# Two of the sixteen weight casts of a fused tanh-multiply matmul are given to VectorE alone

## The chip, the cores and the metric

The kernel runs on one core of a Trainium2 chip, in one launch. The metric is device time in microseconds (us), the median of several runs. Inputs and output lie in the chip's main memory (HBM) as float32.

The engines have these names in the profile: PE is TensorE (matmul), PEld its weight loads, ACT is ScalarE, DVE is VectorE, POOL is GpSimd, SP is SyncE, which here only issues DMAs.

## The reference

```python
def reference(x, w1, w2):          # x: 16 x 512 x 1024, w1 and w2: 1024 x 768
    y1 = np.matmul(x, w1)
    y2 = np.matmul(x, w2)
    return (np.tanh(y1) * y2).astype(np.float32)
```

Flattened, x has 8192 rows: 64 row tiles of 128. The contraction is 1024 = 8 slices of 128.

## The kernel before

**Tiling.** Each weight (`t` = 0 for w1, 1 for w2) is loaded in eight slices of 128 x 768 and cast from float32 to float16 into one tile `wh`. A slice's 768 columns are taken as F = 512 columns and G = 256. A matrix product accumulates eight slices in one of the eight PSUM banks (`bank0` to `bank7`).

**Stages.** The six row tiles 0 to 5 (`HEAD`) and the last (`TAIL`) are computed in the plain way (line 449 issues each matmul, lines 455 and 459 the tanh and the multiplication). The 57 tiles between are taken three at a time, in 19 rounds. Each round computes the three tiles by 15 half-depth products instead of 18, on sums of blocks of x (`A_SUMS`, VectorE, line 434) and on sums of blocks of the weights made once (`B_SUMS`, VectorE, line 424). The products are line 477, the copies and additions between them lines 483 and 492, tanh and multiplication lines 495 and 500. `C_OPS` and `PE_ORDER` fix the order of the products.

**Head.** x tiles 0 to 3 come as float32 and are transposed on PE (line 351). ScalarE moves them out of PSUM with a cast (line 342). PE then goes through the weight slices in the order of their arrival: for every slice `k` it issues F of tiles 0 to 3 (four matmuls of 512 columns) and G of tiles 0 to 3 (four of 256), first for w1 (pass 0), then for w2 (pass 1). Two tiles share a bank for G. So pass 0 holds six banks until ScalarE's tanhs `thF0` to `thF3`, `thG0` to `thG3` have read them, and pass 1 needs six banks itself. Tiles 4 and 5 come as float16 through a casting DMA of GpSimd's queue (line 384) and are transposed on PE (line 361); later tiles are transposed by a DMA (line 387).

**Weights.** The slices are called `a0` to `a7` (w1) and `b0` to `b7` (w2). `a0` to `a3` are loaded by ScalarE's queue, the rest by SyncE's, in order (line 338), through twelve buffers. The casts, `ca0` to `cb7`, are line 344 where VectorE makes them and line 342 where ScalarE does (the same helper `copy`).

**Sums of magnitudes.** ScalarE also sums the absolute values of each x tile (`D0` to `D63`) and of each cast slice (`awa0` to `awb7`), both at line 390. At the end they decide whether the float16 results may stand or a slower general path has to run. GpSimd reuses an x buffer only when its `D` is done.

**Who runs what, and when.** Nothing of the order is written by hand apart from the products of the rounds. A `Planner` holds every operation with the engines that may run it and a time for each, with its due time and its needs. It plays the whole program forward with those assumed times. Where an operation has two engines it is given to the one that can begin earlier, or that is taken first. PSUM banks are dealt in the same play to whatever asks next (`bank_free`). The instructions are then recorded in the order of the planned starts, engine by engine, and kept in that order (`pin`). A cast is entered as `{"dve": 0.5, "act": 0.74}`. Among operations of one engine that could start now or soon, the one with the earlier due time goes first. A cast's due time is `6 + 1.3 * k + 9.5 * t`, that of a tanh of pass 0 is 20, that of `aw` 80 or more.

In the order planned for the kernel before, VectorE has `ca0` to `ca4`, `cb4`, `cb5`, `cb6`, and ScalarE `ca5` to `ca7`, `cb0` to `cb3` and `cb7`.

Of the kernel before, what the change touches and what calls it, by code (L numbers as in the profile page):

```python
# [77 lines left out]
class Planner:  # L78
# [13 lines left out]
    def op(self, name, engines, due, needs, fn, *args, behind=(), issued=(), chains=(), xfer=0.0, latency=None, seeds=False):  # L92


        assert name not in self.ops, name
        self.ops[name] = dict(engines=engines, due=due, needs=[n for n in needs if n], behind=[n for n in behind if n], issued=[n for n in issued if n], fn=fn, args=args,
                              chains=chains, xfer=xfer, latency=latency, seeds=seeds)
        for c in chains:
            self.chains.setdefault(c, {"left": 0, "bank": None, "end": 0.0, "by": ""})["left"] += 1
# [134 lines left out]
def kernel(  # L234
# [29 lines left out]
    LOW, HIGH = 512.0, 1024.0  # L264
    XT_BUFS, S_BUFS, O_BUFS, C_BUFS, WF_BUFS = 4, 2, 3, 2, 12
    WARM = 21
    AFTER = (0, 0, 0)
    SOON = {"S": 3.0, "D": 3.0}
    GATE = 2
# [41 lines left out]
    op = plan.op  # L311
# [229 lines left out]
    for n, what in enumerate(loads):  # L541
# [5 lines left out]
        else:  # L547
            t = "ab".index(what[0])
# [1 line left out]
            op(f"L{what}", {"sp": 0.05}, 0.1 * n - 100, [], load_w, t, i, nc.scalar if what in early else nc.sync,  # L550
               issued=[before], behind=[f"c{slices[j][0]}{slices[j][2]}" if j >= 0 else ""], xfer=xfer)
    for a, t, k in slices:
        op(f"c{a}{k}", {"dve": 0.5, "act": 0.74}, 6 + 1.3 * k + 9.5 * t,
           [f"L{a}{k}"], cast_w, t, k)
        op(f"aw{a}{k}", {"act": 0.92}, 80 + 10 * (t * KO + k), [f"c{a}{k}"], abs_w, t, k)
    for mt in range(4):
# [155 lines left out]
    for mt in range(MT - TAIL - 3):  # L712
        op(f"st{mt}", {"sp": 0.05}, 52 + 4.33 * mt if mt >= HEAD else 250 + 5 * mt, outs[mt], store, mt,
           issued=[f"T{MT - 1}"] if mt < HEAD else [f"p{AFTER[(mt - HEAD) % 3]}.{(mt - HEAD) // 3 + 1}"], xfer=1.1)
    for mt in range(4, MT):
# [23 lines left out]
    pin(nc.vector.memset(ones, 2.0 ** -12))  # L739
    for n in range(WARM):  # L740
        pin(nc.tensor.matmul(banks[n % 8][:, n // 8 % 2 * 2 * P:][:, :2 * P], ones.bitcast(bf16)[:, :P], ones.bitcast(bf16), start=True, stop=True))
# [106 lines left out]
```

## Time and profile before

| | us |
|---|---|
| median of four runs | 300.5 (300.26 to 300.64) |
| the profiled execution, its own time | 300.65 |
| its span, from the first instruction to the last | 298.9 |
| PE busy | 292.1 |
| DVE busy | 240.3 |
| ACT busy | 219.8 |
| POOL busy | 32.9 |

The profile is of one execution. Its span lies inside its own time, so about 1.75 us of that time are outside what the rows show. A row of a timeline gives start, duration, engine, line, operation, written tile <- read tiles, shapes and the number of instructions merged into it. What stands in square brackets is the idle time of the engine before it and what ended that. PE's matmuls overlap: a row's duration is drawn longer than the time from one start to the next. A 512-column matmul is drawn with 0.38 us and starts 0.22 us after the one before it, a 256-column one with 0.27 and 0.11 us.

The granted clock of TensorE is 0.999 over the span. The twelve weight slices of SyncE's queue land, by the trace's stamps, at 13.13, 14.12, 15.12, 16.09 (`a4` to `a7`), 17.05, 18.04, 20.15, 21.13, 22.11, 23.11, 24.06 and 25.19 us (`b0` to `b7`).

### The profile page before, as it was taken

Reading aid. Unit: us, or ns where it says so; the run is one execution under the profiler, and the core shown is the slowest. Engines: PE = TensorE matmul, PEld = TensorE weight load, DVE = VectorE, ACT = ScalarE, POOL = GpSimd, SP = SyncE. Lnnn points to the kernel's source line nnn. Section 1 sums busy time; section 2 is a strip of 40 time slices with the busy share of each in tenths; the row PEclk is TensorE's granted clock in tenths of the full one; section 3 lists DMA queues with packets and bytes.
Section 4 is the critical chain, followed back from the end, with each engine's and each line's share of the span. In section 5 each row is a group of like instructions: output and inputs, shape, how many; then the busy total and the mean of one; then the engine's idle time right before and its main releaser. Section 6 shows DMA issues by size and latency. Waiting matters only on the chain.

```text
span 298.9 us, 4459 instructions
## 1 busy us (share of the span) xinstructions
PE 292.1 (98%) x1418; PEld 138.9 (46%) x1418; DVE 240.3 (80%) x497; ACT 219.8 (74%) x438; POOL 32.9 (11%) x67
## 2 busy tenths in 40 slices
PE   7999999999999999999999999999999999999994
PEld 5656544444444444444444444444444444444452
DVE  1208999988988887888978979797898988888854
ACT  3779989999786868767777767777766777773640
POOL 0021211211101101110110111011011101000000
PEclk9999999999999999999999999999999999999999
DMA  7999999999999999999999999999999999994053
GB/s 281 408 400 210 162 167 152 176 197 244 210 221 206 232 226 145 252 286 147 249 165 274 209 173 252 178 238 198 242 203 194 228 185 267 172 391 158 19 230 124
DMA packets 82585, 64.79 MB, mean 217 GB/s; under 512 B 63617, under 2 KB 64129, under 8 KB 82561
## 3 DMA queue, kind: packets, MB, share of 16 engines
q1 hardware_dynamic: 73344, 47.20, 63.7%
q0 software_dynamic: 8640, 15.73, 36.2%
q10 hardware_dynamic: 576, 1.57, 1.3%
q8 instruction: 11, 0.18, 0.3%
q14 instruction: 14, 0.11, 0.1%
HBM read 39.85 MB, written 25.17 MB: 218 GB/s over the span
## 4 chain that ended last, share of the span: by engine, by line
PE 91%; DMA 6%; ACT 0%; ACTq 0%; DVE 0%; SPq 0%; issue 0%
PE bank L477 82%; PE bank L449 8%; DMA w_f<-in_w_dram 6%; ACTq L338 0%; PE bank L361 0%; ACT wh L342 0%; ACT o L455 0%; DVE o L459 0%; SPq L338 0%; PE bank L515 0%
## 5 line engine op out<-in xcount | busy, mean ns | idle before, releaser
L477 PE MATMUL bank<-b,s 128*128 128x512 f16 x608 | 140.9, 379 | 0.0
L477 PEld LDWEIGHTS <-s 128*128 128x128 f16 x760 | 74.3, 98 | 89.6
L492 DVE TENSOR_TENSOR bank<-bank,s 128x512 f32<-128x512 f32 x95 | 66.0, 695 | 29.2 <-ACT s L483 22.2
L483 ACT ACTIVATE s<-bank 128x512 f32<-128x512 f32 x95 | 55.3, 597 | 42.2 <-PE bank L477 39.3
L390 ACT ACTIVATE junk<-xh 128x1024 f16<-128x1024 f16 x60 | 63.3, 1055 | 0.2
L500 DVE TENSOR_TENSOR o<-o,bank 128x256 f32<-128x256 f32 (+1 forms) x114 | 60.5, 546 | 2.3 <-ACT o L495 1.7
L477 PEld LDWEIGHTS <-xT 128*128 128x128 f16 x380 | 37.2, 98 | 44.7 <-issue 0.2
L477 PE MATMUL bank<-b,xT 128*128 128x512 f16 x228 | 55.4, 379 | 0.0
L384 POOL DMA_DIRECT2D xh<-in_x_dram x60 | 32.1, 535 | 197.9 <-ACT junk L390 149.8
L495 ACT ACTIVATE o<-bank 128x256 f32<-128x256 f32 x76 | 33.1, 437 | 10.1 <-DVE bank L492 6.5
L449 PE MATMUL bank<-wh,xT 128*128 128x512 f16 (+1 forms) x208 | 38.8, 338 | 1.0 <-ACT xT L342 0.7
L477 PE MATMUL bank<-wh,xT 128*128 128x512 f16 x152 | 39.0, 379 | 0.0
L477 PE MATMUL bank<-wh,s 128*128 128x512 f16 x152 | 39.0, 379 | 0.0
L434 DVE TENSOR_TENSOR s<-s,xT 128x512 f16<-128x512 f16 x76 | 31.6, 415 | 0.0
L449 PEld LDWEIGHTS <-xT 128*128 128x128 f16 x208 | 20.0, 98 | 17.9 <-ACT xT L342 1.4
L483 ACT ACTIVATE bank<-bank 128x512 f32<-128x512 f32 x38 | 20.4, 579 | 8.9 <-PE bank L477 7.2
L495 ACT ACTIVATE o<-s 128x512 f32<-128x512 f32 x38 | 23.9, 628 | 2.2 <-DVE s L492 2.0
L344 DVE CAST wh<-w_f 128x768 f16<-128x768 f32 x8 | 4.5, 564 | 18.6 <-DMA w_f<-in_w_dram 18.6
L434 DVE TENSOR_TENSOR s<-xT,xT 128x512 f16<-128x512 f16 x38 | 15.8, 416 | 0.0
L434 DVE TENSOR_TENSOR s<-xT,s 128x512 f16<-128x512 f16 x38 | 15.8, 416 | 0.0
L492 DVE TENSOR_TENSOR bank<-s,bank 128x512 f32<-128x512 f32 x19 | 13.1, 691 | 2.6 <-ACT o L495 2.5
L390 ACT ACTIVATE junk<-wh 128x768 f16<-128x768 f16 x16 | 13.6, 848 | 0.2
(39 smaller groups left out, 121.7 us busy)
## 6 DMA issues: line engine op xcount, KB each, us to landing
out_dram<-o SPq DMA_DIRECT2D x60, 384.0 KB, 4.6
xh<-in_x_dram POOLq DMA_DIRECT2D x60, 256.0 KB, 6.1
w_f<-in_w_dram SPq DMA_DIRECT2D x12, 384.0 KB, 8.1
x_f<-in_x_dram SPq DMA_DIRECT2D x4, 512.0 KB, 7.1
w_f<-in_w_dram ACTq DMA_DIRECT2D x4, 384.0 KB, 7.6
out_dram<-o SPq DMA_DIRECT2D x4, 256.0 KB, 2.5
xT<-xh SPq DMA_TRANSPOSE x58, 5.6
out_dram<-o SPq DMA_DIRECT2D x4, 128.0 KB, 2.1
```

The source lines that it names most:

```text
L344: pin(engine[e].tensor_copy(dst, src))
L384: pin(nc.gpsimd.dma_start(xhs[mt], xf[mt]))
L390: pin(nc.scalar.activation(junk[:, :src.shape[-1]], src, ACT.Abs, scale=scale, accum_out=sums[:, column:column + 1]))
L434: pin(engine[e].tensor_tensor(ss[i, v], x_operand(i, a), x_operand(i, b), OP[how]))
L449: pin(nc.tensor.matmul(b, xts[mt][:, k, :], rhs, start=first, stop=k == KO - 1, skip_group_check=True))
L477: pin(nc.tensor.matmul(place(i, dst), x_operand(i, a)[:, k, :], w_rhs(b, k), start=begins and k == 0, stop=k == KH - 1, skip_group_check=T ...
L483: pin(nc.scalar.activation(d, place(i, src), ACT.Copy, scale=float(sign)))
L492: pin(nc.vector.tensor_tensor(d, a, b, ALU.add if signs == (1, 1) else ALU.subtract))
L495: pin(nc.scalar.activation(out_tile(HEAD + 3 * i + r)[:, lo:lo + n], place(i, src)[:, :n], ACT.Tanh, scale=float(sign)))
L500: pin(nc.vector.tensor_tensor(o, o, place(i, src)[:, at:at + n], ALU.mult))
```

## The change

One constant is added, and the casts of w2's slices with k = 2 and 3 (`cb2` and `cb3`) are entered with VectorE as their only engine. In line 553 of the kernel before, `t` is 1 for w2.

```diff
@@ -264,6 +264,7 @@
     LOW, HIGH = 512.0, 1024.0
     XT_BUFS, S_BUFS, O_BUFS, C_BUFS, WF_BUFS = 4, 2, 3, 2, 12
     WARM = 21
+    ON_DVE = (2, 3)
     AFTER = (0, 0, 0)
@@ -550,7 +551,7 @@
     for a, t, k in slices:
-        op(f"c{a}{k}", {"dve": 0.5, "act": 0.74}, 6 + 1.3 * k + 9.5 * t,
+        op(f"c{a}{k}", {"dve": 0.5} if t and k in ON_DVE else {"dve": 0.5, "act": 0.74}, 6 + 1.3 * k + 9.5 * t,
            [f"L{a}{k}"], cast_w, t, k)
```

Since the planner plays the program anew, more than two casts move. The orders that it gives (`B` is a sum of weight blocks, `S` of x blocks, `mu` a multiplication of the head, `T4` and `T5` the copies of the transposed tiles 4 and 5 out of PSUM; `01F2` is row tile 0, w2, F, slice 2; line numbers behind line 266 are one higher than before):

```
ACT before: ca5 ca6 ca7 cb0 cb1 cb2 cb3 thF0..3 thG0..3 cb7 awa3 D4..D8 D0..D3 thF4 thM4 awa4 ...
ACT after:  ca5 ca6 ca7 cb0 cb1 awa3 thF0..3 thG0..3 cb6 cb7 awa4 D4..D8 D0..D3 thF4 thM4 awa5 ...
DVE before: ca0..ca4 cb4 cb5 cb6 B5 B6 B36 T4 B24 B37 muF0 muF1 T5 muF2 muF3 ...
DVE after:  ca0..ca4 cb2 cb3 cb4 cb5 B5 B6 B36 B24 T4 B37 B26 muF0 muF1 T5 muF2 muF3 ...
PE before:  01F0 11F0 01F1 11F1 01F2 21F0 11F2 21F1 31F0 21F2 01G0 31F1 11G0 21G0 01G1 31G0 ...
PE after:   01F0 11F0 21F0 31F0 01F1 01G0 11F1 11G0 21F1 21G0 31F1 31G0 01G1 11G1 21G1 31G1 01F2 ...
```

PE's order is the same in both from slice 3 of pass 1 on, to the end. SyncE's and GpSimd's orders do not change. ScalarE has one cast fewer on the whole and VectorE one more, since `cb6` goes to ScalarE. `awa4` and every later `aw` move one place forward on ScalarE, up to round 2. VectorE's order differs here and there up to round 4 (`B26`, `B45` and `S21` among others), and the eight banks are dealt differently in some of the rounds.

## The prediction

> **What bounds the kernel now.** I read the page's first lines first, then the chain of waits, then PE's waits, then the timeline around the one place that these name.
>
> ```profile
> span 298.9 us, 4459 instructions
> PE 292.1 (98%) x1418; PEld 138.9 (46%) x1418; DVE 240.3 (80%) x497; ACT 219.8 (74%) x438; POOL 32.9 (11%) x67
> PE 91%; DMA 6%; ACT 0%; ACTq 0%; DVE 0%; SPq 0%; issue 0%
> ```
>
> PE is the bound. A busy PE need not be a PE at its pace, so I compared the starts: from 10.6 us to the last matmul each one starts 0.22 us (512 columns) or 0.11 us (256) after the one before, with a single exception. The list of PE's waits from 10.6 to 280 us agrees; its first line is the exception, its second is the end of a wait at 11.01.
>
> ```profile
> PE bank L449 <- ACT o L455: 0.3, 1, 0.3
> PE bank L449 <- ACT xT L342: 0.2, 1, 0.2
> ```
>
> The chain in order of time shows what ended the first: the fourth slice of w2 lands at 21.13 us, ScalarE casts it, only then makes its first tanh, and PE goes on at 22.53.
>
> ```profile
> 12.77 8.36 DMA w_f<-in_w_dram
> 21.13 0.02 issue
> 21.15 0.83 ACT wh L342
> 21.98 0.51 ACT o L455
> 22.49 0.04 issue
> 22.53 5.58 PE bank L449 x35
> ```
>
> The same place in the timeline:
>
> ```profile
> 20.18 1.81 ACT L342 CAST wh<-w_f 128x768 f16<-128x768 f32 x2 [1.28 <-DMA w_f<-in_w_dram]
> 20.32 3.03 POOL L384 DMA_DIRECT2D xh<-in_x_dram  x5
> 21.89 3.16 ACT L455 ACTIVATE o<-bank 128x512 f32<-128x512 f32 x8
> 22.14 0.56 DVE L344 CAST wh<-w_f 128x768 f16<-128x768 f32 x1 [8.42 <-DMA w_f<-in_w_dram]
> 22.53 2.54 PE L449 MATMUL bank<-wh,xT 128*128 128x512 f16 x15 [0.29 <-ACT o L455]
> ```
>
> The reader is to see two casts of 1.81 us standing ahead of the tanhs, a VectorE that was idle for 8.42 us, and a PE that waits for a bank. The wait is longer than the printed 0.29, which counts from the drawn end of a pipelined matmul. The last start before it is 21.86, the next was due at 21.86 + 0.22 = 22.08 and came at 22.53: **0.45 to 0.46 us** of PE are lost (0.67 between starts, less 0.216). That is all that this change can win on PE. The other late starts lie before 11.1 us, where nothing moves.
>
> **Part 1, the tanhs come earlier.** Without `cb2` and `cb3`, ScalarE is free when `cb1` ends: it starts at 18.07 and takes 0.83, so 18.90. `awa3` now stands next; such a sum took from 25.95 to 26.88 (0.84 and its read-out), so it ends at 19.83. `thF0` needs the last F product of tile 0, which starts at 19.70 and ends 0.38 later. So `thF0` runs from 20.12 to 20.71, and at the 0.48 us spacing of today's tanhs (21.89, 22.38, 22.86) the others end at 21.20, 21.68 and 22.17. PE in its new order starts pass 1 at 21.00 as today and needs those banks at 21.43 (third matmul), 21.65 (fourth), 22.08 (sixth) and 22.73 (tenth). The margins are 0.72, 0.45, 0.40 and 0.56, less some 0.05 for the semaphore. The stall goes: -0.46 us.
>
> **Part 2, the two casts on VectorE.** Two times 0.56 (its row for the same shape), in the idle 8.42 us: 20.16 to 20.72 and 21.14 to 21.70. PE needs `cb2` sixteen matmuls into pass 1, at 21.00 + 8 x 0.216 + 8 x 0.109 = 23.60, and `cb3` at 24.90: margins 2.9 and 3.2. Cost on the path nothing, and it would stay nothing if the casts took ScalarE's 0.83.
>
> **Part 3, `cb6` goes the other way.** It lands at 24.06, ScalarE's last tanh ends before 23.5, so the cast ends at 24.90 (0.83) against 24.64 today. PE needs it at 24.90 + 3 x 1.30 + 0.45 for eight transposes = 29.25. `B36`, which needs `cb7` too, cannot start before that ends at 25.21 + 0.83 = 26.04. VectorE then has `B5` at 23.7, `B6` at 24.9, `B36` at 26.05, `B24` at 27.2 (1.13 each), and `T4`, now behind `B24`, at 28.3 against 28.60 today. PE reads `T4`'s copy at 32.28. At `muF0`, 31.2 against 31.47 today, VectorE already has `B26` behind it, so it is more than a microsecond ahead. Nothing on the path.
>
> **Part 4, does the gain last?** Everything behind must come 0.46 us earlier, or have as much room. ScalarE does not move at first: `cb7` is pinned to its landing at 25.19, and from there ScalarE runs almost without a pause, with the same amount of work as now, to 43.3. There it waits for PE.
>
> ```profile
> 44.17 0.38 ACT L455 ACTIVATE o<-bank 128x256 f32<-128x256 f32 x1 [0.85 <-PE bank L449]
> ...
> 48.51 0.58 ACT L483 ACTIVATE s<-bank 128x512 f32<-128x512 f32 x1
> ...
> 49.15 1.89 PE L477 MATMUL bank<-b,s 128*128 128x512 f16 x8
> ```
>
> The first two rows are ScalarE's, the third is PE's. ScalarE's copy ends at 49.09, 0.06 before the product that waits for it, so this is the tightest spot of the rounds. But the chain to it begins behind the idle 0.85, which a PE that is 0.46 earlier shortens to 0.39. So the copy comes 0.46 earlier too. The x tiles that ScalarE sums and SyncE transposes have at least 0.5 us there (tile 8 lands at 31.14, its sum starts at 31.64), and those sums do not move. VectorE's `add64` starts at 42.66 today and feeds a tanh at 44.45, which may now start at 43.99: room enough. At the end PE stops 0.46 earlier and the same multiplications and stores follow.
>
> **A rule that speaks against it.** Of the five issues on GpSimd between 20.32 and 23.35, the one that a VectorE cast overlapped from 22.14 took 0.80 us, the other late ones 0.54 and 0.55; the cast at 23.14 lengthened nothing. Two more casts now fall beside them, so the x tiles may be issued 0 to 2 x 0.26 = 0.52 us later. Against tile 8's 0.50 that costs ScalarE 0.02, inside its 0.39. If each cast held the queue for its whole 0.56, it would be 1.12, ScalarE 0.62 late, and 0.23 of the gain lost. I take nothing, since the transfers there run one behind the other (tiles 4 to 8 land 1.2 to 1.3 apart) and the queue of loads is not empty before 25.19. The Trainium skill, SBUF — State Buffer, section "SBUF: two separate sides", says that a float32 copy within SBUF on VectorE locks GpSimd out of a shared port, so that it cannot write the descriptors of its DMAs; the next section has 3100 ns for one that alone takes 620. By that page's figures a single delay would be an estimated 2.5 us and the kernel about 1.1 us slower (2.48 - 0.50 - 0.85); the row with 0.80 beside a cast shows a tenth of that.
>
> **Sum.** 300.65 - 0.46 = 300.19 for an execution like the profiled one. The median of the runs shown is 0.15 below that one: **300.05**.
>
> **Rivals.** *No change (the gain is given back).* If ScalarE's chain to 49.09 did not follow PE, or `awa3` pushed `thF2` by more than its 0.40, PE would wait for what it saved. For it: ScalarE is busy 17.77 of the 18.1 us from 25.2. Against it: the idle 0.85. Time 300.5. The casts moving without their effect ends there too.
>
> *Slower.* The banks are dealt anew and VectorE's order differs up to round 4. A hand-over that comes late once per round is paid 19 times: from 0.46 / 19 = 0.024 us a round the gain is eaten, from 0.056 the kernel is slower by 0.2%. At 0.06 it costs 1.1 us: 300.5 - 0.46 + 1.1 = 301.15. For it: VectorE is busy 44.6 of 50 us between 100 and 150. Against it: the nearest hand-over from VectorE there (an addition that ends at 134.89, a product that starts at 135.49) has 0.6 us, ten times as much, and PE's order does not change.
>
> *More than the stall shown.* The stall is set by the landing of `b3`, which the new order no longer needs so early. In runs where it lands later the old kernel loses more. The four runs differ by 0.38; with that the gain is 0.84: 299.66.
>
> **How the numbers follow.** A measurement of this kernel tells about 0.2%, 0.6 us, from no change. Forecast 0.54; more than the stall shown, beyond 0.6 us, 0.28, since 0.14 us more than forecast is enough for it; given back 0.08; slower 0.10. The forecast and the given-back case are both within 0.2%, hence 0.62 there; faster 0.28, slower 0.10. The range goes from 299.6 (0.84 won) to 300.7 (nothing won, and the 0.14 by which the slowest run lies above the median); the slower case is left out.
>
> **What would show it.** In the profile after: no wait of PE for line 456 (tanh) at 22; PE's starts 0.22 and 0.11 apart from 11.1 us on; `thF0` near 20.1; two VectorE casts at 20.2 and 21.1; ScalarE's idle time before 43.7 near 0.4; PE's last matmul near 293.7 where it now starts at 294.3 and ends at 294.56, so 294.1 for the end. I am wrong if PE waits anew between 21 and 60 us, or in every round, or if the x tiles 4 to 8 land more than 0.5 us later.

## The result, and the profile after

| | before | after |
|---|---|---|
| median of all runs, us | 300.64 (60 runs) | 300.15 (40 runs) |
| ratio, with its 95% interval | | 0.9985 (0.9979 to 0.9990) |
| the profiled execution, its own time, us | 300.65 | 300.53 |
| its span, us | 298.9 | 298.8 |

The changed kernel is 0.49 us shorter; the interval makes that 0.30 to 0.63 us. The two profiled executions alone, 0.12 us apart, would have said "no change". Both readings are right, and the reason is in the head. The ratio leaves out one run of each kernel that fell in a slower state (306.64 and 306.24).

The page's first lines after, with PE's line of the chain of waits:

```profile
span 298.8 us, 4463 instructions
PE 292.7 (98%) x1418; PEld 140.0 (47%) x1418; DVE 241.1 (81%) x498; ACT 218.8 (73%) x437; POOL 33.4 (11%) x67
PE 97%; ACT 1%; DVE 0%; issue 0%
```

The 6% of DMA that stood in the chain before are gone: no landing sets the end any more, PE does so from its warm-up on. The list of PE's waits from 10.6 to 280 us has a single line, and the one for the tanh is not in it:

```profile
PE bank L450 <- ACT xT L343: 0.2, 1, 0.2
```

The timeline around the old stall (start, duration, engine, line, operation, tiles, shapes, count; idle time before in brackets):

```profile
16.73 11.43 PE L450 MATMUL bank<-wh,xT 128*128 128x512 f16 x70
18.75 0.84 ACT L391 ACTIVATE junk<-wh 128x768 f16<-128x768 f16 x1
20.42 0.56 DVE L345 CAST wh<-w_f 128x768 f16<-128x768 f32 x1 [6.77 <-DMA w_f<-in_w_dram]
20.45 0.57 POOL L522 COPY held<-w_f 128x1 f32<-128x1 f32 x1 [19.14 <-DMA w_f<-in_w_dram]
20.62 3.17 ACT L456 ACTIVATE o<-bank 128x512 f32<-128x512 f32 x8 [0.94 <-PE bank L450]
20.96 3.13 POOL L385 DMA_DIRECT2D xh<-in_x_dram  x5
21.37 0.61 DVE L345 CAST wh<-w_f 128x768 f16<-128x768 f32 x1 [0.40 <-DMA w_f<-in_w_dram]
24.30 1.78 ACT L343 CAST wh<-w_f 128x768 f16<-128x768 f32 x2 [0.50 <-DMA w_f<-in_w_dram]
```

PE's row runs from 16.73 to 28.16 without a break. ScalarE makes `awa3` (18.75), then waits 0.94 us for PE: the dependence is turned round. The casts `cb2` and `cb3` are VectorE's rows at 20.42 and 21.37, `cb6` is the first of ScalarE's two at 24.30.

But `thF0` starts at 20.62 and not at 20.12. The head of PE, after and then before:

```profile
1.07 4.66 PE L742 MATMUL bank<-ones 128*128 128x256 bf16 x21 [1.07 <-DVE ones L740]
5.52 1.75 PE L352 MATMUL bank<-ident,x_f 128*128 128x128 f32 x8
7.26 0.50 PE L450 MATMUL bank<-wh,xT 128*128 128x512 f16 x2
...
11.52 1.80 PE L450 MATMUL bank<-wh,xT 128*128 128x512 f16 x10 [0.24 <-ACT xT L343]
```

```profile
1.07 4.35 PE L741 MATMUL bank<-ones 128*128 128x256 bf16 x21 [1.07 <-DVE ones L739]
5.28 1.07 PE L351 MATMUL bank<-ident,x_f 128*128 128x128 f32 x8
6.58 0.50 PE L449 MATMUL bank<-wh,xT 128*128 128x512 f16 x2 [0.24 <-ACT xT L342]
...
11.01 1.80 PE L449 MATMUL bank<-wh,xT 128*128 128x512 f16 x10 [0.24 <-ACT xT L342]
```

The same instructions. The first x tile's eight transposes took 1.75 us after, 1.07 before: in the profiled execution of the changed kernel TensorE came to its full pace later (its matmuls start 0.21 us apart up to 6.80 us, then at the pace of 0.11; before, up to 4.88). Its head is 11.52 - 11.01 = 0.51 us late, and that hides the 0.46 us of the stall: the last matmul ends at 294.61 against 294.56. The forty runs, not these two, say what the change is worth. Sorted afterwards by the granted clock, the runs of the changed kernel at 0.999 or more have a median of 300.06, those at 0.998 or less 300.40; for the kernel before, over all its runs beside the experiments, the medians are 300.595 and 300.645 (beside one group of experiments they lie 0.17 apart). That would fit a kernel before that feels a late head less than the changed one does, but it does not show it: the clock is a poor sign of a late head (`replan_alone` below shows 1.0 with a late one, `after_w19` 0.997 with one on time), and the heads of the runs without a profile are not on record. The experiments ask why.

### The profile page after: what moved, and what is told of

The parts are those of the page before. It is cut to its first block, busy times and chain, and to the rows that moved or that the text cites. A ratio compares the mean times of both kernels' runs of the same rounds, so it can differ in the third digit from the quotient of the medians.

```text
span 298.8 us, 4463 instructions
## 1 busy us (share of the span) xinstructions
PE 292.7 (98%) x1418; PEld 140.0 (47%) x1418; DVE 241.1 (81%) x498; ACT 218.8 (73%) x437; POOL 33.4 (11%) x67
## 4 chain that ended last, share of the span: by engine, by line
PE 97%; ACT 1%; DVE 0%; issue 0%
PE bank L478 82%; PE bank L450 12%; PE bank L742 2%; PE bank L352 1%; ACT xT L343 1%; PE bank L362 0%; ACT junk L391 0%; DVE o L460 0%; DVE ones L740 0%; PE bank L516 0%
## 5 line engine op out<-in xcount | busy, mean ns | idle before, releaser
L345 DVE CAST wh<-w_f 128x768 f16<-128x768 f32 x9 | 5.1, 569 | 17.3 <-DMA w_f<-in_w_dram 17.3
```

The lines of the kernel that those rows point to most:

```text
L345: pin(engine[e].tensor_copy(dst, src))
```

## The experiments

Theory: the kernel before is set by the landing of `b3` and then by ScalarE's cast and tanh, so that a late head is swallowed by the stall; the changed kernel is set by PE's unbroken row, which begins with the head. Rivals: the runs differ by chance; the gain comes from the new order and not from the casts; something else in the new order is worth as much as the stall. In every edit `plan` is the finished plan: `start_of` sets the place of an instruction in its engine's order, `engine_of` its engine.

These figures are read out of the profiles of thirteen runs (us; "pace" is the first start of PE behind its last gap of 0.21 us, "x tile 3" the start of the last transpose of the head, "stalls" the time PE lost after 11.3 us):

```
kernel        pace   x tile 3  b3 lands  b7 lands  stalls (at)                     PE end
before        4.88   13.41     21.13     25.19     0.46 (22.53)                    294.56
before_again  6.59   13.76     21.26     25.31     0.24 (22.66)                    294.69
before_w25    5.52   13.78     21.40     25.44     0.36 (22.80)                    294.83
late_tanh     6.37   13.72     21.27     25.33     1.11 (23.50)                    295.52
replan_alone  7.02   13.94     21.31     25.27     0.76 (22.71), 0.27, 0.06        295.72
one_cast      4.25   13.29     21.34     25.38     0.45 (21.76), 0.27              294.70
casts_alone   6.80   13.91     21.49     25.36     none                            294.61
after         6.80   13.92     21.35     25.23     none                            294.61
after_w19     6.27   13.43     21.24     25.12     none                            294.12
after_w17     6.58   13.65     21.25     26.80     0.82 (33.56)                    295.15
after_w25     6.59   14.22     21.33     26.88     0.40 (11.82), 0.33 (33.65)      295.25
before_gate   5.10   13.35     21.20     27.99     0.58 (22.60), 0.59, 0.08, 0.82  296.12
after_gate    3.81   13.43     21.20     28.00     2.25 (34.77)                    296.38
```

Two sums hold in it. In `before`, `before_again` and `before_w25` PE goes on 1.40 us after `b3` landed (22.53 - 21.13, 22.66 - 21.26, 22.80 - 21.40) and ends 272.03 us later, whatever the head did. In `casts_alone`, `after` and `after_w19` PE ends 280.69 or 280.70 us after the last transpose of the head, whatever the landing did. The first kernel follows a DMA, the second its own head.

**The kernel before once more.** The same program; 21 is written as `20 + 1`.

> The kernel before, unchanged, for its single runs with their clocks. Theory (PE waits for tanhs that stand behind the landing of w2's fourth slice): the landing sets the time of PE's restart at 22.53, so it does not matter whether PE came to that spot at once or half a us late. Runs with a granted clock of 0.997 and with 0.999 to 1.000 should then take the same time within 0.1 us, about 300.6, while the changed kernel's runs are 300.05 at 0.999 to 1.000 and 300.48 at 0.997. Rival (clock and stall have nothing to do with each other): here too the runs at 0.997 are about 0.43 us longer than those at 0.999 to 1.000.

Measured: 300.61 (11 runs), ratio 1.0001 (0.9992 to 1.0010). Its head was 0.35 us later than in the first profile (13.76 against 13.41), its stall 0.24 instead of 0.46, with `b3` landing 0.13 later: 0.46 + 0.13 - 0.35. What the head loses is taken out of the stall.

**The casts alone**, without a new plan (on the kernel before):

```diff
     order = plan.run(SOON)
+    plan.engine_of.update(cb2="dve", cb3="dve")
```

> The plan of the kernel before, with its order and its banks, and only the engine of the two casts cb2 and cb3 changed to VectorE. Theory (the two casts in front of the tanhs are the whole cost): all of the gain, 0.5 us under the kernel before, like the changed kernel. Rival (the new order of PE's pass 1 or the newly dealt banks win it): no gain, 0.0.

Measured: 300.38 (12 runs, two at 302.3 and 302.8 that no trace explains), ratio 1.0002 (0.9985 to 1.0019): inconclusive by the time. The five runs at a clock of 1.0 have a median of 300.08, the seven others one of 300.71. The profile speaks plainly; PE's row and ScalarE's tanhs in its timeline:

```profile
14.02 14.14 PE L449 MATMUL bank<-wh,xT 128*128 128x512 f16 x86
...
20.61 3.17 ACT L455 ACTIVATE o<-bank 128x512 f32<-128x512 f32 x8 [1.79 <-PE bank L449]
```

PE's row is unbroken from 14.02 to 28.16, the tanhs wait for PE, and PE ends at 294.61, as in the changed kernel with the same head. The two casts remove the stall in the old order; the rest of the new plan is not needed for it. That their time is the same is not shown.

**The new plan alone**: on the changed kernel, with `cb2` and `cb3` on ScalarE again, ahead of the tanhs.

```diff
     order = plan.run(SOON)
+    plan.engine_of.update(cb2="act", cb3="act")
+    plan.start_of.update(cb2=plan.start_of["thF0"] - 0.02, cb3=plan.start_of["thF0"] - 0.01)
```

> The plan of the changed kernel, with its order of PE, its banks and cb6 on ScalarE, but cb2 and cb3 recorded on ScalarE ahead of the first tanh, as before. Theory: the first tanh runs at 21.98 again, and PE's new order asks for its bank two matmul slots of tile 0 and 1 after 21.00, at 21.43 instead of 22.08. The stall is 22.53 - 21.43 = 1.1 us, 0.65 more than before: about 301.2. Rival (the order wins it): 300.1.

Measured: 301.62 (5 runs, 301.51 to 301.80), ratio 1.0033 (1.0020 to 1.0046). That is 0.98 slower, where 0.6 or so was expected. Three pieces of its chain of waits (start, length, what):

```profile
21.34 0.83 ACT wh L343
22.17 0.99 ACT o L456 x2
...
23.20 6.07 PE bank L450 x37
```

The expectation counted the first tanh. The new order of PE asks for four banks in its first four matmuls of pass 1, so the second tanh is late too: 0.27 us more at 23.20 and 0.06 at 23.69. With the 0.65 that the expectation counts they make the 0.98. The new plan without the casts is worse than no change.

**One cast instead of two**, planned anew:

```diff
-    ON_DVE = (2, 3)
+    ON_DVE = (3,)
```

> Only the fourth slice's cast (k = 3) is VectorE's, planned anew; cb2 stays on ScalarE. Theory: cb2 ends at 21.01, the first tanh runs from 21.02 to 21.61, PE asks for its bank at 21.43 and goes on at 21.66, so 0.2 of the 0.46 us stay lost: 0.25 to 0.3 us under the kernel before. Rival (cb3 alone is the wait, since it is the one whose landing stands in the chain): the whole 0.5.

Measured: 300.61 (12 runs), ratio 1.0012 (0.9998 to 1.0027). Most of the gain that was expected is not there. PE's timeline:

```profile
21.76 6.50 PE L450 MATMUL bank<-wh,xT 128*128 128x512 f16 x38 [0.29 <-ACT o L456]
```

It goes on at 21.76, 1.40 us after `b2` landed (20.36): the same sum, with the slice before. But it pays 0.45 there and again 0.27 for the second tanh, for the reason just seen. The miss is of the same step.

**A tanh made late**: one sum of magnitudes (0.83 us to the next start) stood ahead of `thF0` in the kernel before.

```diff
     order = plan.run(SOON)
+    plan.start_of["awa3"] = plan.start_of["thF0"] - 0.01
```

> The kernel before with one more piece of work ahead of the first tanh on ScalarE: the sum awa3, taken from behind cb7, so ScalarE does the same in all. Theory: the tanhs start 0.96 us later (spacing of two such sums in the profile), PE's bank comes 0.96 later and nothing before the end takes it back: 301.6. Rival (PE's restart at 22.53 is set by something else, the slices' landings, and the tanhs only happen to end then): 300.6 to 300.8.

Measured: 301.39 (8 runs, one of them 312.83), ratio 1.0025 (1.0015 to 1.0036); 0.81 longer than the 300.58 of the runs beside it. Its PE row and two pieces of its chain:

```profile
23.50 5.58 PE L449 MATMUL bank<-wh,xT 128*128 128x512 f16 x35 [0.95 <-ACT o L455]
```

```profile
22.03 0.93 ACT junk L390 x2
22.96 0.49 ACT o L455
```

PE goes on 2.23 us after `b3` landed, 1.40 + 0.83. What is put ahead of the first tanh is paid in full by the kernel. The expectation was about 0.15 too high: the sum of magnitudes with its read-out is a piece of 0.93, but the tanh came only 0.83 later.

**Only the order on ScalarE changed**, the tanhs ahead of the casts:

```diff
     order = plan.run(SOON)
+    tanhs = [f"th{w}{m}" for w in "FG" for m in range(4)]
+    for n, name in enumerate(tanhs):
+        plan.start_of[name] = plan.start_of["cb2"] - 0.01 + 0.001 * n
```

> The kernel before with the eight tanhs of pass 0 recorded ahead of cb2 and cb3, all still on ScalarE. Theory: the tanhs run from 20.1 to 23.3, but then cb2 ends near 24.1 and PE, which asks for it at 21.86, waits 2.2 us instead of 0.46: about 302.4. Both casts have to leave ScalarE for the gain. Rival (the order on ScalarE is all): 300.1.

Measured: 301.39 (8 runs). As it came out, the tanhs stand ahead of the products of slice 7 of pass 0 as well: they leave that slice out of w1's product, so this kernel computes something else, and those products wait for them (five stalls of 0.04 to 0.34 from 19.93 to 22.01). It does not answer its question. Whether an order on ScalarE alone could do what the casts do stays open.

**The head made longer**: four more warm-up matmuls, on the kernel before and on the changed one.

```diff
-    WARM = 21
+    WARM = 25
```

> The kernel before with 25 warm-up matmuls instead of 21, so that PE's real work begins 0.44 us later (four at 0.109 us) or up to 0.85 later where the clock is still not granted. Theory (the landing of w2's fourth slice sets PE's restart, and an earlier PE only waits longer): the 0.44 is absorbed in the stall of 0.46, and runs with the clock granted early stay at 300.6; those with a late grant, which reach the spot late already, lose some tenths: median 300.6 to 300.9. Rival (PE's own work is the bound throughout): 0.44 longer, 301.05.

> The changed kernel with 25 warm-up matmuls instead of 21. Theory: nothing is left to absorb a late PE, so it pays the whole delay, 0.44 us where the clock is granted early: 300.5 to 300.6 there, 300.8 to 300.9 with a late grant, and the change's gain over the kernel before with 25 is nearly gone. Rival: it stays 0.5 under the kernel before with 25.

Measured: before_w25 300.65 (12 runs), ratio 1.0002 (0.9992 to 1.0012): swallowed. after_w25 300.32 (11 runs), ratio 0.9993 (0.9985 to 1.0002), 0.17 above the changed kernel where about 0.44 was expected. PE in the timeline of before_w25:

```profile
22.80 5.58 PE L449 MATMUL bank<-wh,xT 128*128 128x512 f16 x35 [0.19 <-ACT o L455]
```

In this profile the head is 0.37 us later than in the first and `b3` lands 0.27 later. The stall falls from 0.46 to 0.36, and PE ends 0.27 later, by the landing alone: the head's delay is absorbed. The runs of after_w25 fall in two groups, 300.05 to 300.35 and 300.91 to 301.21; the profile is of the second, and there a late `b7` costs 0.33 beside the late head, as is told with the next pair. The direction is as expected, the size is not settled by it.

**The head made shorter**, on the changed kernel:

```diff
-    WARM = 21
+    WARM = 19        # after_w19
+    WARM = 17        # after_w17
```

> The changed kernel with 19 warm-up matmuls. Theory: in the runs with a late grant (the profile of the changed kernel is one) PE is still warming up at 5.52 while the first x tile has landed at 4.99, and each warm-up matmul costs 0.21 there; two fewer win up to 0.4 in those runs, so that they come to 300.1 as well, and nothing in those with an early grant, where x lands at 5.14 and PE comes to it at 5.28. Median 300.05 instead of 300.15, and no two groups any more. Rival (with less warm-up the clock is granted later still, and the head loses it again): late runs at 300.5 or longer, or more of them.

> The same with 17 warm-up matmuls. Theory: they end before the first x tile lands (17 at 0.213 from 1.07 are 4.7), so nothing more is won than with 19: 300.05. Rival (the idle time before x's first transposes delays the grant): late runs longer than with 19, by up to 0.11 us for each matmul that then runs at half pace.

Measured: after_w19 300.24 (12 runs), ratio 0.9984 (0.9968 to 1.0001); after_w17 300.47 (12 runs), ratio 0.9988 (0.9967 to 1.0010). Of both 300.05 was expected. Neither can be told from the changed kernel, so no better version comes out of it. The profile of after_w19 is useful, because its head happens to be on time (x tile 3 at 13.43). Two rows of ScalarE:

```profile
20.13 3.17 ACT L456 ACTIVATE o<-bank 128x512 f32<-128x512 f32 x8 [0.39 <-PE bank L450]
...
43.73 0.38 ACT L456 ACTIVATE o<-bank 128x256 f32<-128x256 f32 x1 [0.48 <-PE bank L450]
```

With PE on time the tanhs start at 20.13 and PE ends at 294.12, 0.44 before the kernel before. The profile of after_w17 shows a weak spot of the new order:

```profile
26.82 0.83 ACT L343 CAST wh<-w_f 128x768 f16<-128x768 f32 x1 [1.46 <-DMA w_f<-in_w_dram]
27.68 2.36 DVE L425 TENSOR_TENSOR b<-wh 128x2048 f16<-128x2048 f16 x2 [1.60 <-ACT wh L343]
30.56 2.35 DVE L425 TENSOR_TENSOR b<-wh,b 128x2048 f16<-128x2048 f16 x2
32.83 1.28 DVE L460 TENSOR_TENSOR o<-o,bank 128x512 f32<-128x512 f32 x2
33.56 5.34 PE L450 MATMUL bank<-wh,xT 128*128 128x512 f16 x24 [0.65 <-DVE o L460]
```

Here `b7` landed at 26.80 instead of 25.2. ScalarE casts it at 26.82, VectorE stands 1.60 idle for it, makes its four sums (`B36`, `B24`, then `B37`, `B26`, the copy `T4` between the pairs) and only then `muF0`, which is 1.3 us late (32.83 against 31.53); PE loses 0.82. The profile of after_w25 shows the same with 26.88 and 0.33. In both, the slices show a gap of more than two microseconds ahead of `b3`, not ahead of `b2`: `b2` landed at 18.79 and 18.87, and `b3` at its usual 21.25 and 21.33. GpSimd's x loads are let go by `b2`'s landing (`held`, line 522). The next pair asks whether that is the link.

**The x loads let go one slice earlier**, on both kernels:

```diff
-        pin(nc.gpsimd.tensor_copy(held, wfs[1, GATE][:, :1]))
+        pin(nc.gpsimd.tensor_copy(held, wfs[1, GATE - 1][:, :1]))
```

> The kernel before, with GpSimd's loads of x tiles 4 to 8 let go when w2's second slice lands (18.0) instead of the third (20.2); the plan is not changed. They then share the DMA engines with the last weight slices, and b7 should land 1 to 2 us later, near 26.8, as it did in the profiles of the two changed kernels with 25 and 17 warm-up matmuls, where b2 landed at 18.8. Theory (VectorE's new order is what a late b7 hurts, since B36, which needs b7, now has B24 ahead of T4 and B26 ahead of the first multiplication): the old order has one sum of weight blocks less before that multiplication, PE waits there 0 to 0.3 us at most, and the kernel stays at 300.6 to 300.9. Rival (a late b7 costs both orders the same): 0.3 to 0.8 us longer, 300.9 to 301.4.

> The changed kernel with the same. Theory: the first multiplication comes near 33 instead of 31.5, and PE waits 0.3 to 1.0 us for its bank near 33.5: 300.6 to 301.2, no better than the kernel before with the same loads, and in some runs worse. Rival (VectorE is a microsecond ahead and takes the late slice): 300.15.

Measured: before_gate 302.23 (5 runs, 301.68 to 302.66), ratio 1.0050 (1.0037 to 1.0063); after_gate 302.15 (6 runs), ratio 1.0058 (1.0036 to 1.0079). `b7` landed at 28.0 in both, 2.8 us late, so the link holds: x loads let go earlier push the last slice back. It is more than expected, and it cost the kernel before 1.5 us where almost nothing was expected. PE's rows of before_gate, then two rows of after_gate:

```profile
33.62 5.34 PE L449 MATMUL bank<-wh,xT 128*128 128x512 f16 x24 [0.43 <-DVE o L459]
...
50.70 1.67 PE L477 MATMUL bank<-b,s 128*128 128x512 f16 x7 [0.66 <-ACT s L483]
```

```profile
28.89 2.36 DVE L425 TENSOR_TENSOR b<-wh 128x2048 f16<-128x2048 f16 x2 [2.55 <-ACT wh L343]
...
34.77 5.34 PE L450 MATMUL bank<-wh,xT 128*128 128x512 f16 x24 [2.08 <-DVE o L460]
```

At `muF0` the old order loses 0.59 and the new one 2.25, for two reasons: VectorE has one more sum (`B26`) between `b7` and the multiplication, which starts 1.15 us later (34.03 against 32.88), and PE, without the stall at 22.60, is there half a microsecond earlier. But the old order pays again at 50.70, 0.82, where ScalarE's chain from `b7` comes late, and keeps its stall at 22.60. The totals are the same. A late `b7` eats the whole gain of the change.

## Why the prediction was right, and where it was not

**The sum.** Forecast 300.05 and a gain of 0.45 on the median shown; measured 300.15 and 0.49. The likeliest case came, at its size, inside the 0.2% that one measurement cannot tell from no change; with sixty and forty runs the interval (0.30 to 0.63) leaves out a gain of nothing. The level was 0.10 too low because the median of four runs that it starts from, 300.5, lies 0.14 under that of the sixty. The mechanism is shown from both sides: `casts_alone` takes the stall away (in its profile; its time alone could not tell), `late_tanh` makes it longer by what it puts in the way, in profile and time.

**The 0.46 us.** Right as a reading of one execution, wrong as a constant. The step "the other late starts lie before 11.1 us, where nothing moves" took PE's arrival as fixed. The head varies, the old stall is `b3`'s landing + 1.40 less that arrival (0.24 to 0.46 in three profiles), and what is won is that difference. Sorted by the clock, a poor sign of the head, it is 0.54 (300.595 to 300.06) and 0.25 (300.645 to 300.40). The 0.49 comes out of a mix of heads. That it lies so near to 0.46, the largest stall of those three profiles, is partly luck.

**Part 1.** `thF0` was to start at 20.12: 20.62 in the profile after, 20.13 in `after_w19`, whose head was on time. The margins held, but they rest on the order of the banks; `replan_alone` and `one_cast` showed that when the first tanh is late, the second is as well, and my expectations for these two left that term out.

**Part 2.** The casts took 0.56 and 0.61 at 20.42 and 21.37 and hid, as predicted.

**Part 3.** "Nothing on the path" holds while `b7` lands by about 25.4 (three profiles without a stall). With 26.8 it costs 0.33 to 0.82, with 28.0 2.25. The cover was smaller than the prediction has it ("more than a microsecond ahead"). In the profile after, VectorE goes from `B26` into `muF0` without a pause:

```profile
31.53 1.28 DVE L460 TENSOR_TENSOR o<-o,bank 128x512 f32<-128x512 f32 x2
```

`muF0` ends at 32.21, such a bank is handed on 0.05 later (33.51 to 33.56 in `after_w17`), and PE asks for it at 33.01: 0.75 us of cover. In `after_w17`, `muF0` is 1.30 late and PE 0.27 earlier, so 0.82 is lost. A `b7` that is 1.6 us late came in the profiles with 17 and 25 warm-up matmuls and not in the one of the changed kernel itself.

**Part 4.** PE was to end at 294.1 and ScalarE's idle time to be 0.39: 294.61 and 0.85 in the profile after, 294.12 and 0.48 in `after_w19`. PE loses nothing after 11.6 us in the profile after beyond 0.02 at 51.8. The spot named as the tightest, ScalarE's copy at 49.15, is the one that broke in `before_gate`.

**The rule on GpSimd.** The row after shows `held`'s copy at 0.57; the same copy before:

```profile
20.20 0.18 POOL L521 COPY held<-w_f 128x1 f32<-128x1 f32 x1 [18.89 <-DMA w_f<-in_w_dram]
```

A VectorE cast ran beside it after (20.42 to 20.98), none before. The prediction looked for the delay in the five issues, and there it was small: one took 0.89 after where one took 0.80 before. The first x issue came 0.64 later, of which 0.25 is `b2`'s own landing (20.40 against 20.15) and 0.39 this copy, a term that the prediction does not have. Tile 8 landed at 31.61 against 31.14. That is within the bound of 0.52, but by other terms than its own, so this was luck; it cost nothing on the path. The estimated 2.5 us that the figures of the Trainium skill would make (SBUF — State Buffer, section "A bandwidth-pool intuition that's wrong (but worth ruling out)") were not seen.

**The rivals.** "The gain is given back at 49.15" did not come: no PE wait is there. "Slower, banks dealt anew" fell: no round of the profile after shows a PE stall. "More than the stall shown" was right that the kernel before hangs on `b3`'s landing, and wrong on the size: in these three profiles of its order `b3` landed within 0.27 us (21.13 to 21.40), and the head, later in the two with the later landing, took part of that back (stalls of 0.24 and 0.36 there, not more than 0.46).

**Open.** Why a few runs of `casts_alone` and `one_cast` are two microseconds longer, and when the slices' gap falls ahead of `b2` or of `b3`.

## What to carry to other kernels

A stall that waits for a landing also swallows whatever is late ahead of it. When it is removed, those delays come to light, and one profile of each kernel can show no gain where forty runs show one; compare the starts of the first common instruction before the ends. When a tanh frees a bank, count the banks that the next matmuls ask for and not the first alone.

## What the runs showed of the hardware

The point at which matmul starts went from 0.21 to 0.11 us apart lay anywhere from 3.81 to 7.02 us in these profiles, in programs whose first microseconds on PE are the same but for the number of warm-up matmuls. TensorE was busy from 1.07 us in all of them. The granted clock does not show it: in the profile after it reads 1.00 in each of the first nine microseconds. The Trainium skill, TensorE: Matmul & The Clock Gate, section "Part 1: The HAM clock gate (the "warmup" mystery)", says that the clock is raised after a busy window of about 3.4 us and that this window runs freely, so that the point depends on where the first matmul falls in it. The spread seen here, 7.02 - 3.81 = 3.21, is of the size of one such window; the page's own figure for the variation, 500 ns either way, is too small for these runs.

The landings of SyncE's slices are 0.98 us apart, but in every profile there is a gap of more than two microseconds, ahead of `b2` or of `b3`: 18.04 to 20.15 (`b1` to `b2`) in the kernel before, 18.79 to 21.25 (`b2` to `b3`) in `after_w17`. The DMA engines do not pause in it: in the kernel before they move 378 and 396 GB/s in the two microseconds from 18 to 20. When the x loads of GpSimd's queue were let go earlier, the last slices came later: in `after_gate`, `b6` landed at 25.80 instead of 24.27, and `b7`, issued 2.1 us before the first of these loads (16.13 against 18.20), at 28.00 instead of 25.23.

A copy of one column on GpSimd took 0.57 us in the five profiles in which a float32 cast of VectorE had just begun beside it (`after`, `casts_alone`, and the changed kernel with 17, 19 and 25 warm-up matmuls), and 0.18 or 0.19 in the nine others.
